# A decoder layer on one core: TensorE sums the last block's squares at the boundaries itself, and two planned waits get shorter

## The chip, the core and the metric

One NeuronCore of a Trainium2 chip runs the whole kernel. The metric is the device time of one execution in microseconds; the median of three executions is 1598.87 us (1598.24 to 1599.2). The core has a matrix engine (TensorE, PE in the profile, with its weight loads as PEld), three engines for elementwise work (VectorE or DVE, ScalarE or ACT, GpSimd or POOL), and SyncE (SP), which here issues DMAs. Each engine takes its instructions in order; between engines they wait for one another by semaphores.

## The reference

One layer of a decoder for 512 prompt tokens and 8 x 4 sample tokens, model width 1024, all in float32, with an RMS norm before and after each of three sub-layers and a shift, scale and gate from a conditioning vector:

```
x += 1/2 * gate1 * post1( SwiGLU1( mod1(pre1(x)) ) )
h  = mod2(pre2(x)); p = h @ w_in
   branch A: gated DeltaNet (conv, decay, delta rule)    branch B: sliding-window attention
   y = sigmoid(gate_A) * o_A + sigmoid(gate_B) * o_B
x += gate2 * post2( y @ w_out )
x += 1/2 * gate3 * post3( SwiGLU2( mod3(pre3(x)) ) )

def rmsnorm(x, gain):
    y = x * lax.rsqrt(jnp.mean(x * x, axis=-1, keepdims=True) + EPS)
    return y * gain
```

What bears on the change is the mean of squares over the 1024 features of a token, at each post and each pre norm after the first.

## The kernel before

Activations lie transposed, features on partitions: 8 blocks of 128 features by 544 tokens (`xT`). The tokens are worked in two halves of 272 (TH), c = 0 and c = 1; the second half holds the 32 sample tokens. A matrix product in float32 is made of three matmuls: weights arrive by DMA (`raw`), ScalarE rounds them to `hi`, VectorE or GpSimd forms `lo` = raw - hi (line 271), and `mm3` (line 301) adds hi x xh, hi x xl and lo x xh in PSUM. In the profile `pd` is the down projection of a feed-forward network, `pg` and `pu` are its gate and up projections, `pb` the projections of the mixer, `adaps` the projection of the conditioning vector.

A sub-layer's output is gathered in `dacc` block by block. After each block `sumsq` (line 516) squares it on ScalarE (`sqt`), and adds the square to `sqd`, a tile of 128 partitions by 544 tokens: blocks 0 to 6 on GpSimd, block 7 on VectorE (line 525). When block 7 is done, `boundary` (line 578) is started for that half of the tokens. It runs in this order:

- `rms` (line 357) on `sqd`: three matmuls with 128 tokens of `sqd` as weights against a column block of ones sum over the partitions (`post_s`, line 366); VectorE forms mean plus EPS (`rmsx`) and eleven small steps of a reciprocal square root (`rms3y`, `rms3a`, lines 334 to 345); TensorE turns the roots round and spreads them over the partitions (`post_p`, lines 353 and 355).
- `residual` (line 555): for each block VectorE forms `mt` and adds it to `xT`, ScalarE squares the new `xT`, and the square is added to `sqx`, blocks 0 to 6 on GpSimd, block 7 on VectorE.
- `rms` on `sqx` (`pre_s`, `pre_p`), then `modulate` (line 527), which makes the split input `hh`, `hl` of the next projection.

This happens twice for each half: after the first feed-forward network (about 440 to 520 us) and after the mixer (about 1130 to 1190 us). In the program the norms are called post2, pre3, post5 and pre6. The end of the layer (`Last.finish`, line 761, about 1542 us for c = 0 and 1579 us for c = 1) has the sums and roots of post8 and then the outputs `yo`. `xnps` and `dnps` are transposes for the output.

The order of the instructions is written by a planner, `Streams` (line 145). The main stream of projection units runs, and side streams, such as a boundary, are taken up when they are due: each `yield cost, latency` adds cost to a model clock and makes the stream due again after 1.5 times the latency. So the latency of a yield says how many units of the main stream are put between two steps of a side stream. In `rms` the yield between sums and transposes is `yield 0.7, 3.0`; in `residual` each block has `yield 0.0, 0.8`; between residual and the second norm stands `yield 0.0, 1.0`. GpSimd also clears tiles for the mixer's inverse (`X`, `XL`, lines 1389 and 1390), of which `X` waits for the last `mt` of the first boundary.

Of the kernel before, what the change touches and what calls it, by code (L numbers as in the profile page):

```python
# [19 lines left out]
P = 128  # L20
# [26 lines left out]
NDOWN = 7  # L47
NFRONT = 5
# [188 lines left out]
class Layer:  # L237
# [118 lines left out]

    def rms(self, sq, cs, name):


        nc = self.nc  # L360
        ps = self.wk(name + "_s")
        n = 3 * len(cs)
        s3 = ps[:, :n * 64].rearrange("p (c n) -> p c n", n=64)
        for i, c in enumerate(cs):
            for j, o in enumerate((0, P, TH - P)):
                nc.tensor.matmul(out=s3[:, 3 * i + j, :], lhsT=sq[:, c * TH + o:c * TH + o + P], rhs=self.ones[:, :64],
                                 start=True, stop=True)
        x = self.st.tile([P, 6], F32, tag="rmsx", name="rmsx")[:, :n]
        nc.vector.tensor_scalar(out=x, in0=s3[:, :, 0], scalar1=1.0 / D, scalar2=EPS, op0=ALU.mult, op1=ALU.add)
        r = self.rsqrt(x, [P, n], "rms%d" % n)  # L370
        yield 0.7, 3.0
        out = []
        e = 2 * P - (TH - P)
        for i in range(len(cs)):
            rp = self.wk(name + "_p")
            self.bcast_cols(r, [(3 * i, 0, P), (3 * i + 1, 0, P), (3 * i + 2, e, P)],
                            [rp[:, :P], rp[:, P:2 * P], rp[:, 2 * P:TH]], name)
            out.append(rp[:, :TH])
        yield 0.6, 0.4
        return out  # L380
# [134 lines left out]

    def sumsq(self, x, sq, b, tmp, c, eng=None):

        nc = self.nc
        s = slice(c * TH, (c + 1) * TH)
        if b == 0:  # L520
            nc.scalar.activation(out=sq[:, s], in_=x[:, s], func=AF.Square)
        else:
            t = tmp.tile([P, TH], F32, tag="v", name="sqt", bufs=V_BUFS)
            nc.scalar.activation(out=t, in_=x[:, s], func=AF.Square)
            (eng or nc.gpsimd).tensor_tensor(out=sq[:, s], in0=sq[:, s], in1=t, op=ALU.add)

# [28 lines left out]
    def residual(self, rp, d, gseg, tmp, sqx, c):  # L555

        nc = self.nc
        o, n = c * TH, TH - c * NS
# [8 lines left out]
        for b in range(8):  # L567
            t = tmp.tile([P, TH], F32, tag="u", name="mt", bufs=U_BUFS)
            nc.vector.scalar_tensor_tensor(out=t[:, :n], in0=d[:, b, s], scalar=self.modT[:, gseg, b, 0:1],
                                           in1=rp[:, :n], op0=ALU.mult, op1=ALU.mult)  # L570
            nc.vector.tensor_tensor(out=self.xT[:, b, s], in0=self.xT[:, b, s], in1=t[:, :n], op=ALU.add)  # L571
            self.sumsq(self.xT[:, b, :], sqx, b, tmp, c, nc.vector if b == 7 else None)
            yield 0.0, 0.8

    def boundary(self, sqd, d, gseg, seg, tmp, sqx, x, c, done, after=None):

        rp, = yield from self.rms(sqd, (c,), f"post{gseg}")
        yield from self.residual(rp, d, gseg, tmp, sqx, c)
        if after:
            after(c)  # L580
        yield 0.0, 1.0
        rp, = yield from self.rms(sqx, (c,), f"pre{seg}")
        yield from self.modulate(rp, seg, tmp, x, c)
        done.add(c)


    def ffn(self, pre, x, env, front, ndown, hook, each=None):
# [3 lines left out]
        nc, a = self.nc, self.a  # L591
# [63 lines left out]
        def down(half, b, cs):  # L655
# [3 lines left out]
            for k0 in (0, 4, 8):  # L659
                def go(w, k0=k0):  # L660
# [16 lines left out]
                    for c in cs:  # L677
                        self.sumsq(d[:, b, :], sqd, b, tmp, c, nc.vector if b == 7 else None)
                        if each:
                            each(b, c)  # L680
                        if b == 7:
                            hook(c)
                nk = 4 if k0 < 8 else 3
# [30 lines left out]
class Last:  # L714
# [45 lines left out]

    def finish(self, c, pss):
        nc, L, a = self.nc, self.L, self.L.a
        ps = L.wk("post8_s")
        s3 = ps[:, :192].rearrange("p (c n) -> p c n", n=64)
        for i, o in enumerate(self.OFF):
            nc.tensor.matmul(out=s3[:, i, :], lhsT=self.sqd[:, c * TH + o:c * TH + o + P], rhs=L.ones[:, :64],
                             start=True, stop=True)
        v = L.st.tile([P, 3], F32, tag="rmsx", name="rmsx")
# [1023 lines left out]
def layer(ctx, tc, a, dbg=None, stop=None):  # L1792
# [19 lines left out]

    def hook1(c):
        sch.spawn(L.boundary(sqd, env["d"], 2, 3, tmp, sqx, x, c, done), c)

# [47 lines left out]
    def main():  # L1863
# [23 lines left out]
        def useh(b, c):  # L1887
            def f(ps):
                dd, sq, t = bufs["d"], bufs["sqd"], bufs["tmp"]
                nc.scalar.copy(out=dd[:, b, c * TH:(c + 1) * TH], in_=ps[:, c, :TH])  # L1890
                L.sumsq(dd[:, b, :], sq, b, t, c, nc.vector if b == 7 else None)
                if b == 7:
                    sch.spawn(L.boundary(sq, dd, 5, 6, t, bufs["sqx"], x, c, done,
                                         lambda c: sch.spawn(last[0].turn_x(c), 2)), c)
            return f
# [43 lines left out]
        last.append(Last(L, tmp, d, bufs["sqd"], hp, fp))  # L1939
        feed.add(L.ffn("ffn2", x, bufs, NFRONT, NDOWN, lambda c: sch.spawn(last[0].finish(c, last[0].ps), 0), last[0].block))  # L1940
        yield from feed.run(mo)
# [34 lines left out]
```

## Time and profile before

| | before |
|---|---|
| median of three executions | 1598.87 us (1598.24 to 1599.2) |
| the profiled execution, its own time | 1593.05 us |
| its span, first to last instruction | 1591.2 us |
| mean granted clock of TensorE | 0.985 |
| TensorE busy | 1517.3 us (95%) |
| VectorE busy | 853.9 us (54%) |
| ScalarE busy | 633.7 us (40%) |
| GpSimd busy | 288.3 us (18%) |

The profile is of one execution. An engine's busy share is an average over stages with different limits. In a row of a timeline the first number is the start within the span, the second the length, `x3` the number of instructions drawn together, and the bracket the idle time before them with what ended it. The granted clock 1.00 is TensorE's full speed, 2.4 GHz; a mean below it over a stretch is a share of the stretch at 1.2 GHz.

### The profile page before, as it was taken

How to read it: one execution, taken by the hardware profiler on the slowest of the kernel's cores; microseconds unless marked ns; L12 is line 12 of the kernel's file. 1: busy time of each engine (PE TensorE's matmuls, PEld its weight loads, DVE VectorE, ACT ScalarE, POOL GpSimd, SP SyncE). 2: the span in 40 equal slices, each digit the busy share in tenths (PEclk: the TensorE clock that was granted, in tenths of full speed). 3: DMA queues.
4: the chain of work that ended last, by engine and by line, in shares of the span. 5: the costliest groups of instructions: out<-in, count | busy, mean ns of one | idle time of the engine just before them, and what ended most of it. 6: DMA issues, size and time to landing. Idle time of an engine off the chain costs nothing. (4 is left out here: it accounts for less than half of the span.)

```text
span 1591.2 us, 32547 instructions
## 1 busy us (share of the span) xinstructions
PE 1517.3 (95%) x12851; PEld 1406.0 (88%) x12851; DVE 853.9 (54%) x2080; ACT 633.7 (40%) x1397; POOL 288.3 (18%) x395
## 2 busy tenths in 40 slices
PE   7999999999998999999999998998979999999996
PEld 3799999999987999997788997897979999999995
DVE  5433322333588778578789556756474332233365
ACT  4322222322445553455485242233455332223363
POOL 2000000000343232131021023131548000000042
PEclk9999999999999999999999999999999999999998
DMA  9564445455556434753112324614425432333253
GB/s 317 162 193 134 152 142 157 141 159 157 173 158 189 119 82 100 174 143 85 45 44 68 93 81 126 179 49 133 139 67 161 108 87 86 91 90 90 80 154 112
DMA packets 314528, 199.66 MB, mean 125 GB/s; under 512 B 36596, under 2 KB 297295, under 8 KB 314086
## 3 DMA queue, kind: packets, MB, share of 16 engines
q1 hardware_dynamic: 314086, 197.46, 43.8%
q8 instruction: 101, 1.65, 0.4%
q14 instruction: 53, 0.43, 0.1%
q0 software_dynamic: 288, 0.11, 0.0%
HBM read 182.08 MB, written 16.36 MB: 125 GB/s over the span
## 5 line engine op out<-in xcount | busy, mean ns | idle before, releaser
L270 ACT CAST hi<-raw 128x512 fp32r<-128x512 f32 (+2 forms) x502 | 287.9, 581 | 608.9 <-PE pu L301 171.6
L271 DVE TENSOR_TENSOR lo<-raw,hi 128x512 fp32r<-128x512 f32 (+2 forms) x368 | 253.7, 690 | 391.8 <-ACT hi L270 383.1
L301 PE MATMUL pb<-hh,hi 128*128 128x272 f32 (+1 forms) x1008 | 233.6, 302 | 4.1 <-ACT hh L270 3.0
L301 PE MATMUL pb<-hl,hi 128*128 128x272 f32 (+1 forms) x1008 | 225.5, 293 | 3.2 <-DVE hl L271 3.2
L271 POOL TENSOR_TENSOR lo<-raw,hi 128x512 fp32r<-128x512 f32 (+1 forms) x104 | 137.0, 1321 | 498.0 <-ACT hi L270 465.2
L301 PE MATMUL pb<-hh,lo 128*128 128x272 f32 (+1 forms) x1008 | 224.1, 293 | 0.2
L301 PEld LDWEIGHTS pb<-hh,hi 128*128 128x128 f32 (+1 forms) x1008 | 163.7, 190 | 16.9 <-issue 7.2
L301 PE MATMUL pd<-fh,hi 128*128 128x272 f32 x704 | 172.0, 291 | 0.0
L301 PE MATMUL pd<-fl,hi 128*128 128x272 f32 x704 | 170.7, 289 | 0.0
L301 PEld LDWEIGHTS pb<-hl,hi 128*128 128x128 f32 (+1 forms) x1008 | 164.2, 190 | 5.4 <-DVE hl L271 3.6
L301 PE MATMUL pd<-fh,lo 128*128 128x272 f32 x672 | 163.1, 290 | 3.3 <-DVE lo L271 2.7
L301 PEld LDWEIGHTS pb<-hh,lo 128*128 128x128 f32 (+1 forms) x1008 | 162.9, 190 | 2.3 <-DVE lo L271 0.8
L301 PE MATMUL pg<-hh,hi 128*128 128x272 f32 x672 | 150.0, 293 | 7.3 <-ACT hh L538 3.6
L301 PE MATMUL pu<-hh,hi 128*128 128x272 f32 x672 | 148.4, 291 | 0.0
L301 PE MATMUL pg<-hl,hi 128*128 128x272 f32 x672 | 147.1, 290 | 0.3 <-DVE hl L539 0.2
L301 PE MATMUL pu<-hl,hi 128*128 128x272 f32 x672 | 146.4, 289 | 0.0
L301 PE MATMUL pu<-hh,lo 128*128 128x272 f32 x672 | 145.5, 288 | 0.7 <-POOL lo L271 0.7
L301 PE MATMUL pg<-hh,lo 128*128 128x272 f32 x672 | 145.6, 288 | 0.0
L301 PEld LDWEIGHTS pd<-fh,hi 128*128 128x128 f32 x704 | 120.5, 189 | 8.6 <-issue 4.2
L301 PEld LDWEIGHTS pg<-hh,hi 128*128 128x128 f32 x672 | 109.0, 189 | 20.3 <-issue 5.0
L301 PEld LDWEIGHTS pd<-fl,hi 128*128 128x128 f32 x704 | 120.9, 189 | 0.0
L301 PEld LDWEIGHTS pd<-fh,lo 128*128 128x128 f32 x672 | 114.6, 189 | 5.1 <-DVE lo L271 3.7
(455 smaller groups left out, 2510.6 us busy)
## 6 DMA issues: line engine op xcount, KB each, us to landing
raw<-w_in SPq DMA_DIRECT2D x136, 256.0 KB, 3.1
wa<-w_ada SPq DMA_DIRECT2D x56, 512.0 KB, 4.3
raw<-ffn_w_gate SPq DMA_DIRECT2D x94, 256.0 KB, 2.9
raw<-ffn_w_up SPq DMA_DIRECT2D x94, 256.0 KB, 2.9
raw<-ffn_w_down SPq DMA_DIRECT2D x92, 256.0 KB, 3.0
wb<-w_ada SPq DMA_DIRECT2D x32, 256.0 KB, 6.3
S<-state_delta SPq DMA_DIRECT2D x8, 512.0 KB
delta_sample<-S SPq DMA_DIRECT2D x8, 512.0 KB, 5.4
```

The costliest lines, as they stand in the source:

```text
L270: self.nc.scalar.copy(out=hi, in_=raw)
L271: (eng or self.nc.vector).tensor_tensor(out=lo, in0=raw, in1=hi.bitcast(F32), op=ALU.subtract)
L301: self.nc.tensor.matmul(out=ps[:m, c, :TH], lhsT=a[:r, kt, :m], rhs=b[:r, kx, c * TH:(c + 1) * TH], start=first and i == 0, stop=last and ...
```

## The change

At block 7 the square is no longer added to `sqd` or `sqx`. It stays in its own tile, and `rms` gets it as `extra`: after each of the three sum matmuls a second one with `extra` as weights adds into the same columns of PSUM. This holds at ten places: post2, pre3, post5, pre6 and post8, each for both halves. So ten additions on VectorE are gone (six into `sqd`, four into `sqx`) and thirty matmuls are new. The first norm of the kernel is as before. Three latencies of the planner are smaller: 3.0 to 2.0 between sums and transposes, 0.8 to 0.7 for each block of the residual, 1.0 to 0.6 between residual and second norm. They apply to the boundaries; with them, and since the plan's clock runs otherwise, the steps of the boundaries stand at other places among the projections.

```diff
@@ def rms
-    def rms(self, sq, cs, name):
+    def rms(self, sq, cs, name, extra=None):
...
                 nc.tensor.matmul(out=s3[:, 3 * i + j, :], lhsT=sq[:, c * TH + o:c * TH + o + P], rhs=self.ones[:, :64],
-                                 start=True, stop=True)
+                                 start=True, stop=extra is None)
+                if extra is not None:
+                    nc.tensor.matmul(out=s3[:, 3 * i + j, :], lhsT=extra[:, o:o + P], rhs=self.ones[:, :64],
+                                     start=False, stop=True)
...
-        yield 0.7, 3.0
+        yield 0.7, 2.0
@@ def sumsq
-    def sumsq(self, x, sq, b, tmp, c, eng=None):
+    def sumsq(self, x, sq, b, tmp, c, eng=None, alone=False):
...
             nc.scalar.activation(out=t, in_=x[:, s], func=AF.Square)
+            if alone:
+                return t
             (eng or nc.gpsimd).tensor_tensor(out=sq[:, s], in0=sq[:, s], in1=t, op=ALU.add)
@@ def residual, def boundary
-            self.sumsq(self.xT[:, b, :], sqx, b, tmp, c, nc.vector if b == 7 else None)
-            yield 0.0, 0.8
-
-    def boundary(self, sqd, d, gseg, seg, tmp, sqx, x, c, done, after=None):
-
-        rp, = yield from self.rms(sqd, (c,), f"post{gseg}")
-        yield from self.residual(rp, d, gseg, tmp, sqx, c)
+            t = self.sumsq(self.xT[:, b, :], sqx, b, tmp, c, alone=b == 7)
+            yield 0.0, 0.7
+        return t
+
+    def boundary(self, sqd, extra, d, gseg, seg, tmp, sqx, x, c, done, after=None):
+
+        rp, = yield from self.rms(sqd, (c,), f"post{gseg}", extra)
+        t = yield from self.residual(rp, d, gseg, tmp, sqx, c)
         if after:
             after(c)
-        yield 0.0, 1.0
-        rp, = yield from self.rms(sqx, (c,), f"pre{seg}")
+        yield 0.0, 0.6
+        rp, = yield from self.rms(sqx, (c,), f"pre{seg}", t)
         yield from self.modulate(rp, seg, tmp, x, c)
         done.add(c)
@@ def ffn, after a block of the down projection
-                        self.sumsq(d[:, b, :], sqd, b, tmp, c, nc.vector if b == 7 else None)
+                        t = self.sumsq(d[:, b, :], sqd, b, tmp, c, alone=b == 7)
...
-                            hook(c)
+                            hook(c, t)
@@ Last.finish
-    def finish(self, c, pss):
+    def finish(self, c, pss, extra):
...
-                             start=True, stop=True)
+                             start=True, stop=False)
+            nc.tensor.matmul(out=s3[:, i, :], lhsT=extra[:, o:o + P], rhs=L.ones[:, :64], start=False, stop=True)
@@ the output of the mixer, and the three places that start a boundary or the end, hand the tile on
-                L.sumsq(dd[:, b, :], sq, b, t, c, nc.vector if b == 7 else None)
+                e = L.sumsq(dd[:, b, :], sq, b, t, c, alone=b == 7)
...
```

Two places in the new order. VectorE at the end of the modulation of half 0 at the first boundary, about 482 to 490 us in the profile before; `mt` and `hl` belong to the modulation, `dacc` is the accumulation of a block of half 1, `sqd` the addition of its last square, and `rmsx` the first step after the sum of post2 of half 1. Before:

```order
L536 SCALAR_TENSOR_TENSOR mt<-xT,modT,pre_p 128x272 x3
L539 SCALAR_TENSOR_TENSOR hl<-mt,modT,hh 128x272 x3
L271 TENSOR_TENSOR lo<-raw,hi 128x512
L536 SCALAR_TENSOR_TENSOR mt<-xT,modT,pre_p 128x272
L676 TENSOR_TENSOR dacc<-pd,dacc 128x272
L539 SCALAR_TENSOR_TENSOR hl<-mt,modT,hh 128x272
L525 TENSOR_TENSOR sqd<-sqd,sqt 128x272
L369 TENSOR_SCALAR rmsx<-post_s 128x3
```

After:

```order
L544 SCALAR_TENSOR_TENSOR hl<-mt,modT,hh 128x272 x2
L541 SCALAR_TENSOR_TENSOR mt<-xT,modT,pre_p 128x272 x3
L271 TENSOR_TENSOR lo<-raw,hi 128x512
L544 SCALAR_TENSOR_TENSOR hl<-mt,modT,hh 128x272 x3
L682 TENSOR_TENSOR dacc<-pd,dacc 128x272 x2
L372 TENSOR_SCALAR rmsx<-post_s 128x3
```

Both last accumulations into `dacc` now stand behind the modulation, directly ahead of the root, and the addition is gone.

GpSimd at the end of the residual of half 1 at the first boundary, about 500 to 510 us before; `sqx` are the additions of the squares of blocks 1 to 5 and of block 6, `X` and `XL` the tiles that are cleared for the mixer, `lo` a subtraction for a block of weights. Before:

```order
L271 TENSOR_TENSOR lo<-raw,hi 128x512 x3
L525 TENSOR_TENSOR sqx<-sqx,sqt 128x272 x5
L1389 MEMSET X 128x1024
L525 TENSOR_TENSOR sqx<-sqx,sqt 128x272
L1390 MEMSET XL 128x512
L271 TENSOR_TENSOR lo<-raw,hi 128x512
```

After:

```order
L271 TENSOR_TENSOR lo<-raw,hi 128x512
L530 TENSOR_TENSOR sqx<-sqx,sqt 128x272 x5
L1396 MEMSET X 128x1024
L1397 MEMSET XL 128x512
L271 TENSOR_TENSOR lo<-raw,hi 128x512
L530 TENSOR_TENSOR sqx<-sqx,sqt 128x272
```

The addition of block 6 now stands behind both clearings and a subtraction; before, only the first clearing stood ahead of it.

## Rows read from the trace of the kernel before

**Rows 1.** The page, busy time, share of the span and instructions of each engine:

```profile
PE 1517.3 (95%) x12851; PEld 1406.0 (88%) x12851; DVE 853.9 (54%) x2080; ACT 633.7 (40%) x1397; POOL 288.3 (18%) x395
```

**Rows 2.** The view of line 525: who waited for its additions (us, times):

```profile
  PE post_s L366: 3.4, 3
...
  PE post_s L766: 2.1, 2
  PE pre_s L366: 2.1, 1
```

**Rows 3.** Stretches: length, busy time (instructions), PEclk, share of DMA, GB/s:

```profile
460.00:470.00 10.00, 8.48 (x49) 7.51 (x49) 8.63 (x15) 5.79 (x15) 7.01 (x7) 0.83 0.57 164
...
1170.00:1180.00 10.00, 6.19 (x31) 5.25 (x30) 9.41 (x16) 6.14 (x13) 7.39 (x9) 0.68 0.38 105
```

**Rows 4.** Timeline of PE, 443 to 471 us: start, length, [idle before]; then by line, 440 to 480:

```profile
443.07 0.88 PE L366 MATMUL post_s<-ones,sqd 128*128 128x64 f32 x6 [0.24 <-DVE sqd L525]
...
448.61 0.38 PE L353 MATMUL post_p<-ident,rms3y 128*128 128x128 f32 x2
...
470.54 0.78 PE L366 MATMUL pre_s<-ones,sqx 128*128 128x64 f32 x6
471.13 0.37 PE L301 MATMUL pd<-fh,hi 128*128 128x272 f32 x1
...
L301 PE MATMUL pd<-fh,lo 128*128 128x272 f32 x72 | 21.8, 303 | 2.2 <-DVE lo L271 2.1
```

**Rows 5.** Timeline of DVE, 446 us:

```profile
446.25 1.22 DVE L343 SCALAR_TENSOR_TENSOR rms3a<-rmsx,rms3y 128x3 f32<-128x3 f32 x1
```

**Rows 6.** Timeline of POOL, 446 us:

```profile
446.16 1.29 POOL L271 TENSOR_TENSOR lo<-raw,hi 128x512 fp32r<-128x512 f32 x1 [5.44 <-ACT hi L270]
```

**Rows 7.** Timeline of PE, 485 to 494 us:

```profile
485.66 1.05 PE L467 MATMUL adaps<-wa,cT 128*32 128x512 f32 x4 [1.10 <-DMA wa<-w_ada]
...
493.83 0.43 PE L353 MATMUL post_p<-ident,rms3y 128*128 128x128 f32 x2 [1.16 <-DVE rms3y L345]
```

**Rows 8.** Timeline of DVE, 477 to 487 us:

```profile
477.70 1.31 DVE L536 SCALAR_TENSOR_TENSOR mt<-xT,modT,pre_p 128x272 f32<-128x272 f32 x3 [0.24 <-PE pre_p L355]
...
486.41 0.50 DVE L539 SCALAR_TENSOR_TENSOR hl<-mt,modT,hh 128x272 fp32r<-128x272 f32 x1 [0.24 <-ACT hh L538]
```

**Rows 9.** Timeline of PE, 509 to 514 us:

```profile
509.20 0.88 PE L366 MATMUL pre_s<-ones,sqx 128*128 128x64 f32 x6 [2.06 <-DVE sqx L525]
...
513.70 0.43 PE L353 MATMUL pre_p<-ident,rms3y 128*128 128x128 f32 x2 [0.30 <-DVE rms3y L345]
```

**Rows 10.** Timeline of POOL, 507 to 510 us:

```profile
507.00 0.95 POOL L1389 MEMSET X<- 128x1024 f32 x1 [0.70 <-DVE mt L569]
507.91 0.76 POOL L525 TENSOR_TENSOR sqx<-sqx,sqt 128x272 f32<-128x272 f32 x1
508.61 0.53 POOL L1390 MEMSET XL<- 128x512 f32 x1
509.09 1.27 POOL L271 TENSOR_TENSOR lo<-raw,hi 128x512 fp32r<-128x512 f32 x1
```

**Rows 11.** Timeline of PE at the second boundary, 1136 to 1189 us:

```profile
1136.53 0.88 PE L366 MATMUL post_s<-ones,sqd 128*128 128x64 f32 x6 [1.69 <-DVE sqd L525]
...
1156.02 0.88 PE L366 MATMUL post_s<-ones,sqd 128*128 128x64 f32 x6 [1.47 <-DVE sqd L525]
...
1176.39 0.59 PE L301 MATMUL pg<-hh,hi 128*128 128x272 f32 x1 [1.69 <-ACT sil L607]
...
1183.55 0.77 PE L366 MATMUL pre_s<-ones,sqx 128*128 128x64 f32 x6
...
1189.24 0.43 PE L353 MATMUL pre_p<-ident,rms3y 128*128 128x128 f32 x2 [0.25 <-DVE rms3y L345]
```

**Rows 12.** Timeline of POOL, 1135 us:

```profile
1135.22 0.77 POOL L525 TENSOR_TENSOR sqd<-sqd,sqt 128x272 f32<-128x272 f32 x1
```

**Rows 13.** Timeline of DVE, 1579 us:

```profile
1578.95 0.44 DVE L525 TENSOR_TENSOR sqd<-sqd,sqt 128x272 f32<-128x272 f32 x1 [0.57 <-ACT sqt L524]
```

More of the change, by code (lines that the diff above doesn't have):

```diff
@@ L1811, in layer, with hook1 @@
     done = set()
-    def hook1(c):
-        sch.spawn(L.boundary(sqd, env["d"], 2, 3, tmp, sqx, x, c, done), c)
+    def hook1(c, t):
+        sch.spawn(L.boundary(sqd, t, env["d"], 2, 3, tmp, sqx, x, c, done), c)
     env = {"tmp": tmp, "sqd": sqd}
@@ L1890, in f @@
                 nc.scalar.copy(out=dd[:, b, c * TH:(c + 1) * TH], in_=ps[:, c, :TH])
-                L.sumsq(dd[:, b, :], sq, b, t, c, nc.vector if b == 7 else None)
+                e = L.sumsq(dd[:, b, :], sq, b, t, c, alone=b == 7)
                 if b == 7:
-                    sch.spawn(L.boundary(sq, dd, 5, 6, t, bufs["sqx"], x, c, done,
+                    sch.spawn(L.boundary(sq, e, dd, 5, 6, t, bufs["sqx"], x, c, done,
                                          lambda c: sch.spawn(last[0].turn_x(c), 2)), c)
@@ L1939, in main @@
         last.append(Last(L, tmp, d, bufs["sqd"], hp, fp))
-        feed.add(L.ffn("ffn2", x, bufs, NFRONT, NDOWN, lambda c: sch.spawn(last[0].finish(c, last[0].ps), 0), last[0].block))
+        feed.add(L.ffn("ffn2", x, bufs, NFRONT, NDOWN, lambda c, t: sch.spawn(last[0].finish(c, last[0].ps, t), 0), last[0].block))
         yield from feed.run(mo)
```

## The prediction

> **What bounds the kernel now.** I read the page's busy line first: TensorE is busy for 1517.3 of 1591.2 us, VectorE for 853.9, GpSimd for 288.3 [rows 1]. On the whole TensorE is the bound, so work that is moved from VectorE to TensorE costs its full price unless it fills time in which TensorE stood idle. Second, I asked the view by line what follows the additions that the change takes off VectorE: TensorE waited for them 3.4 us at the layer's own sums of squares after a projection, 2.1 us at those of the last stage and 2.1 us at those ahead of a projection, 7.6 us at six of the ten places [rows 2]. That is what there is to win directly. Third, the table by stretches tells which engine is full around the places: from 460 to 470 us VectorE is busy 8.63 of 10 us and the granted clock is 0.83; from 1170 to 1180 VectorE is busy 9.41, TensorE 6.19, clock 0.68 [rows 3]. So at the boundaries, and only there, VectorE sets the pace, and a wait that goes at a sum can come back a few microseconds on. The rest of the reading is the timeline at each place.
>
> **The price of the added work.** At each of ten places three more matmuls of 128x128 against 64 columns are issued. Three of the same shape, each with weights of its own, stand at 470.54, and the next matmul at 471.13 [rows 4]: 0.59 us. No row shows one that accumulates; with the same shape and weight loads I take 0.6 us a place, 6.0 us in all (5.9 by this row, 6.9 by the 0.69 us that the places after a wait show, where the first records are stretched). The row counts two records for each matmul. The Trainium skill, FP8 and Floating Point Precision, section TensorE Precision Notes, counts four passes for a true fp32 matmul; 30 matmuls of four passes of 64 columns at 2.4 GHz would be 3.2 us by that (an estimate). It would make the sum below 2.8 us lower, but the interval between starts is measured, and the weights have to be loaded too, so the row decides.
>
> **First boundary, token half 0.** The sum at 443.07 waited 0.24 us for the addition [rows 4]. It goes, but the Square on ScalarE is still needed, so it is all that is won there. The transposes that bring the roots back (448.61 [rows 4]) now stand twelve matmuls sooner in the order, 1.5 us at 0.127 us each (38 of them lie between 443.76, where the three sums were issued, and 448.61). The roots' chain on VectorE cannot follow: its ninth step, from 446.25, lasts 1.22 us, as long as a subtraction that GpSimd runs from 446.16 to 447.45 [rows 5, 6], and with two steps more the chain is done at 447.9 whether it begins a little sooner or not. TensorE would be there at about 447.5, so it waits up to 0.4 us; I take half. Term: +0.6 - 0.24 + 0.2 = +0.6. The residual on VectorE begins about 1 us sooner, but in the new order a split of 0.85 us and one more pair of its operations stand ahead of the next weights; the waits for weights that total 2.1 us between 440 and 480 [rows 4] stay as they are by that count: 0, with -2.1 (all gone) and +1.0 as bounds. The drop of the clock there costs 1.7 us (0.17 of 10 us at half speed [rows 3]); it may go with them. The sum at 470.54 waited for nothing: +0.6.
>
> **First boundary, half 1.** The order moves its first sum from behind two groups of adaLN matmuls to a place ahead of them. Before, TensorE waited 1.10 us for the DMA of those weights and 1.16 us for the roots [rows 7]. In the new order VectorE does both last accumulations into dacc behind the whole modulation of half 0, and the Square of block 6 and its addition on GpSimd follow them. The modulation began at 477.70 and with its last operation ended at 486.9 [rows 8]; now its sum stands ten matmuls sooner, and six matmuls and a pair of the adaLN ones (1 us) no longer stand between sum and transposes: 3.0 us less the 0.6 that the sum itself takes, so it begins 2.4 us sooner, with 0.3 us more of splits in it. It ends at 484.8, dacc is done at 485.2, and with a Square of 0.43 us (an estimate by VectorE's operations of that size) and an addition of 0.77 the sum is ready at about 486.5. TensorE stood at the DMA's wait from 484.5 [rows 7]; the new place is nine matmuls ahead, 1.1 us, and the terms so far delay it by 1.2: 484.6. So a new wait of 1.9 us (0.9 to 3.0), in which the DMA's is hidden, takes the place of the 2.26 us: +0.6 - 2.26 + 1.9 = +0.2. The second sum waited 2.06 us at 509.20 [rows 9]. Its chain was: VectorE's last mt, GpSimd's memset of X (0.95 us, which waits for this mt since it takes over its input's memory), the addition of block 6 (0.76), then the one removed (0.44) [rows 10]. In the new order two more operations of GpSimd stand ahead of block 6's addition: the memset of XL (0.53) and a weight subtraction (1.27) [rows 10]. From the start of the memset to the sum that makes 0.95 + 0.53 + 1.27 + 0.76 = 3.5 us, where it was 2.2 (507.00 to 509.20 [rows 9, 10]): the removed 0.44 us is paid three times over. Against this the residual begins some 3.9 us sooner (transposes at 490 instead of 493.83), so its last mt falls between 499 and 501.3, the sum is ready between 502.6 and 504.9, and TensorE, which was there at 507.14, with the sum some 45 matmuls further up (5.7 us) and 1.4 us of delay, at 502.8: a wait of 0 to 2.1, I take 1.0. The transposes then wait 0.7 instead of 0.30 us [rows 9], as fewer matmuls stand between. Term: +0.6 - 2.06 + 1.0 + 0.4 = 0, between -1.0 and +1.1.
>
> **Second boundary.** The sum at 1136.53 waited 1.69 us [rows 11], but block 6's addition on GpSimd, behind three weight subtractions in its queue, ended only at 1135.99 [rows 12]. So it starts 0.5 us sooner, not 1.2, and loses that to its own 0.6 us. At 1156.02 the wait of 1.47 us [rows 11] is filled by the other half's sums, which the new order puts ahead. All this lies before a stretch that VectorE bounds: TensorE goes on at 1176.39, after 1.69 us for ScalarE's sil [rows 11], which in the new order has one more Square of the residual ahead of it. What is won or lost before falls into that wait: I count +0.3 for the whole stretch up to there (-1.0, if VectorE's two additions of 0.44 us go straight through, to +0.8). At 1183.55 nothing waited [rows 11], and nothing covers the new matmuls: +0.6. The transposes at 1189.24 waited 0.25 us [rows 11] and stand ten rows of work, 1.2 us, sooner, while the chain starts 0.6 us later and meets GpSimd's subtractions as it did at 446 [rows 5, 6]: a wait of about 0.9 instead of 0.25, of which some comes back at a later wait: +0.4. Together +1.0.
>
> **The tail.** At half 0, 1542 us, the smaller of the two waits of 2.1 us [rows 2] pays for the 0.6 us, and a split that moves inside the roots' chain keeps the outputs where they were: 0 (-1 to +1.5). At half 1 nothing follows but the roots and the output. VectorE's addition from 1578.95 to 1579.39 goes [rows 13], and TensorE's sums begin right after the Square, at 1578.9. The three transposes that stood between the sums go behind them, which about pays for the three matmuls: -0.45, the length of the addition.
>
> **The sum.** 0.6 + 0 + 0.6 + 0.2 + 0 + 0.3 + 1.0 + 0 - 0.45 = +2.25 us. On the profiled execution (1593.05 us) that is 1595.3. The median of the runs shown is 5.8 us higher than this execution; the change's terms are the same there: 1598.87 + 2.25 = 1601.1, which is 0.14% more. A difference under 0.2% (3.2 us) cannot be told from none here.
>
> **Rivals.** (a) The waits go and nothing takes their place: 6.0 - 7.6 for the sums, -0.45 at the end as the chain there is VectorE's, and of the 3.8 us of waits and low clock around 460 us about half, since VectorE is rid of two additions and the roots come sooner: -4, at 1595. For it speaks that six of ten places show the wait; against it, that at 1136 and at 509 GpSimd ends last once VectorE's addition is gone. Chance 0.25. (b) Slower: GpSimd's addition of block 6 behind the memsets and the subtraction. Where the last mt falls at 501.3, TensorE waits 2.1 us, not 1.0, and together with the new wait of 2 to 3 us before it the stretch from 484 to 505 has few full microseconds. Around 463 us three waits of this size were followed by a mean clock of 0.83 over ten microseconds [rows 3]; the same again is 1.7 us. The Trainium skill, TensorE: Matmul & The Clock Gate, section A second HAM failure mode, says that short idle times between groups of matmuls make the clock go to and fro between its two levels; the two windows of rows 3 agree. With 1.1 + 1.7 on the sum, and 0.4 more at the transposes of 1189: +5.5, at 1604.3. It decides from a wait above 2 us at the second sum of half 1. Chance 0.33. (c) The forecast, that gains and added work cancel within 3.2 us: 0.42; by itself 1597 to 1602. (That the change doesn't do what it says, in that the order shifts nothing but adds the work, is 6.0 - 7.6 and a few tenths: within (c).)
>
> The range reaches from most of (a) to most of (b): 1594.5 to 1605.5. Faster by over 0.2% 0.25, within 0.2% 0.42, slower by over 0.2% 0.33.
>
> **What would show it.** In the profile after: TensorE's busy time up by about 6 us; VectorE's down by some 4 (ten times 0.44); no wait of TensorE for VectorE's sqd or sqx at the sums, but waits for GpSimd's additions at 509 and 1136 and for a Square or GpSimd at the first sum of half 1; the roots' transposes waiting longer than before; the last roots 0.45 us sooner after the last accumulation. I am wrong if the second sum of half 1 waits for nothing, if the clock does not fall around 463 any more, or if the resumption at 1176 comes more than a microsecond sooner or later against the stretch before it.

## The result, and the profile after

| | before | after |
|---|---|---|
| median of four executions | 1599.03 us (1598.24 to 1602.68) | 1613.75 us (1612.61 to 1615.17) |
| the profiled execution, its own time | 1593.05 us | 1612.61 us |
| mean granted clock | 0.985 | 0.978 |

The ratio is 1.009 (95% interval 1.0072 to 1.0108): 14.7 us slower, above the range of the prediction. (Executions of the kernel before, in this and the later comparisons, spread from 1593 to 1606 us, and the first profile of it is of a short one. So whole kernels are compared by several executions of each, and single profiles stretch by stretch.)

The page's busy line of after, which answers to [rows 1]:

```profile
PE 1532.1 (95%) x12911; PEld 1421.6 (88%) x12911; DVE 849.0 (53%) x2070; ACT 634.3 (39%) x1397; POOL 290.3 (18%) x395
```

VectorE lost its ten additions (853.9 to 849.0 us), TensorE has 60 more records (two for each of 30 matmuls). Its busy time grew by 14.8 us, not by the 6 of the new matmuls: where the granted clock is at 1.2 GHz, a matmul is busy for longer (0.43 instead of 0.29 us in the rows below).

To see where the time went I took the start of the same matmul in both traces and subtracted. After lies 0.3 us behind before at 480 us and 0.1 at 500, then 7.1 at 530, 6.8 at 560; 12.1 at 1110 and 13.8 at 1130; 17.9 at 1240; 18.2 at 1535 and 19.8 at the end. After was already 0.6 us behind at 435, so the first boundary (435 to 560) costs 6.2 us, and all of it falls between 500 and 530; the second (1130 to 1240) costs 4.1 and the tail 1.6. The rest arises in the mixer, where both kernels have the same instructions in the same order (taken up below, with a second profile of each).

TensorE at the second sum of half 1 of the first boundary, which answers to [rows 9] (start, length, then in the bracket the idle time before the row and what ended it):

```profile
505.97 0.69 PE L366 MATMUL pre_s<-ones,sqx 128*128 128x64 f32 x2 [4.40 <-POOL sqx L530]
506.45 0.63 PE L369 MATMUL pre_s<-ones,sqt 128*128 128x64 f32 x2
...
508.16 0.64 PE L369 MATMUL pre_s<-ones,sqt 128*128 128x64 f32 x2
508.55 0.57 PE L301 MATMUL pb<-hh,lo 128*128 128x272 f32 x1
508.93 0.43 PE L301 MATMUL pb<-hh,hi 128*128 128x272 f32 x1
```

TensorE came to the sum at 501.57 and stood for 4.40 us, where it had waited 2.06 before. What follows runs at half the clock: six matmuls from 505.97 to 508.55 (2.58 us; six take 1.25 to 1.3 at full clock, as below), and projections 0.23 us apart instead of 0.13 up to 512.10. The stretches show it (length, busy time and instructions of PE, PEld, DVE, ACT, POOL, then the granted clock, DMA share, GB/s):

```profile
500.00:510.00 10.00, 5.45 (x28) 5.01 (x27) 5.23 (x13) 2.76 (x7) 5.82 (x8) 0.77 0.78 285
510.00:520.00 10.00, 9.29 (x65) 8.75 (x63) 7.83 (x26) 5.56 (x13) 0.90 (x2) 0.89 0.34 88
```

The same two stretches before:

```profile
500.00:510.00 10.00, 7.84 (x61) 7.40 (x60) 8.30 (x14) 5.91 (x14) 8.99 (x10) 1.00 0.55 139
510.00:520.00 10.00, 9.70 (x78) 8.79 (x78) 8.74 (x32) 5.03 (x13) 1.77 (x6) 1.00 0.84 290
```

GpSimd at the same place, which answers to [rows 10]:

```profile
500.88 1.30 POOL L530 TENSOR_TENSOR sqx<-sqx,sqt 128x272 f32<-128x272 f32 x1 [0.93 <-ACT sqt L527]
502.12 0.95 POOL L1396 MEMSET X<- 128x1024 f32 x1
503.01 0.52 POOL L1397 MEMSET XL<- 128x512 f32 x1
503.50 1.26 POOL L271 TENSOR_TENSOR lo<-raw,hi 128x512 fp32r<-128x512 f32 x1
504.72 1.20 POOL L530 TENSOR_TENSOR sqx<-sqx,sqt 128x272 f32<-128x272 f32 x1
```

The first row is the addition of block 5, which itself stood 0.93 us for a Square. From there on there is no gap: from 502.12 to 505.92 GpSimd is busy with what the new order put ahead of block 6's addition, and with the addition, which takes 1.20 us, not 0.76, while VectorE runs a subtraction of 1.48 us beside it. All waits of TensorE above 0.3 us between 440 and 540 us sum to 6.8 us before and 7.8 after: the waits did not go, they were gathered into one.

The second boundary, which answers to [rows 11]. TensorE of after:

```profile
1148.43 0.43 PE L366 MATMUL post_s<-ones,sqd 128*128 128x64 f32 x2 [0.39 <-POOL sqd L530]
...
1191.93 0.59 PE L301 MATMUL pg<-hh,hi 128*128 128x272 f32 x1 [2.58 <-ACT sil L613]
...
1205.04 0.43 PE L353 MATMUL pre_p<-ident,rms3y 128*128 128x128 f32 x2 [1.42 <-DVE rms3y L345]
...
1218.60 0.39 PE L301 MATMUL pg<-hh,hi 128*128 128x272 f32 x1 [1.40 <-ACT sil L613]
```

The waits at the sums are gone or small (0.39 instead of 1.69 and 1.47), and three later ones have grown: for `sil` 2.58 (1.69 before) and 1.40 (0.49), for the roots of half 1 1.42 (0.25). All above 0.3 us from the first sum on: 9.8 us before, 11.2 after. The clock is down for longer: 0.83, 0.91 and 0.75 in the three tens from 1170 to 1200, where before had 0.68, 0.98 and 1.00. The new matmuls are 0.66 us a place (four places, 2.6 us).

The tail: at half 0 a new wait of TensorE, for a split of weights on VectorE that now stands behind two outputs `yo` in a row; it was 0.31 us before. VectorE's split, then TensorE:

```profile
1569.11 1.75 DVE L271 TENSOR_TENSOR lo<-raw,hi 128x512 fp32r<-128x512 f32 x1
...
1570.91 0.40 PE L301 MATMUL pd<-fh,lo 128*128 128x272 f32 x1 [2.28 <-DVE lo L271]
```

At half 1, VectorE from the last accumulation to the first step of the root, where [rows 13] had its addition; first before, then after:

```profile
1577.94 0.44 DVE L676 TENSOR_TENSOR dacc<-pd,dacc 128x272 f32<-128x272 f32 x1 [2.91 <-PE pd L301]
...
1580.65 0.16 DVE L769 TENSOR_SCALAR rmsx<-post_s 128x3 f32<-128x3 f32 x1 [1.16 <-PE post_s L766]
```

```profile
1597.71 0.44 DVE L682 TENSOR_TENSOR dacc<-pd,dacc 128x272 f32<-128x272 f32 x1 [2.91 <-PE pd L301]
...
1600.03 0.16 DVE L776 TENSOR_SCALAR rmsx<-post_s 128x3 f32<-128x3 f32 x1 [1.19 <-PE post_s L774]
```

2.71 us before, 2.32 after. So 0.39 us are won there.

### The profile page after: what moved, and what is told of

It reads as the page before. It is cut to its first block, busy times and chain, and to the rows that moved or that the text cites. A ratio compares the mean times of both kernels' runs of the same rounds, so it can differ in the third digit from the quotient of the medians.

```text
span 1610.8 us, 32652 instructions
## 1 busy us (share of the span) xinstructions
PE 1532.1 (95%) x12911; PEld 1421.6 (88%) x12911; DVE 849.0 (53%) x2070; ACT 634.3 (39%) x1397; POOL 290.3 (18%) x395
## 4 chain that ended last, share of the span: by engine, by line
PE 78%; DVE 11%; DMA 4%; ACT 2%; issue 2%; POOL 2%; SPq 0%; DVEq 0%; ACTq 0%; POOLq 0%
PE pb L301 18%; PE pg L301 16%; PE pu L301 15%; PE pd L301 14%; PE adaps L470 3%; DVE y L1202 1%; DVE lo L271 1%; PE psc L1017 1%; DMA raw<-ffn_w_down 1%; PE pgu L301 1%; PE pov L1073 1%; POOL lo L271 1%; PE pkq L1289 1%; ACT hi L270 1%; DVE X L1430 1%
```

## The experiments

Below, "behind" is always the start of the same matmul minus that in the first profile of before, what a boundary costs is read between the same times as above, and medians are compared with those of before on the same chip (1599.7 in the first two sets, 1600.0 in the third).

**The new sums with the old latencies.** In the kernel after:

```diff
-        yield 0.7, 2.0
+        yield 0.7, 3.0
-            yield 0.0, 0.7
+            yield 0.0, 0.8
-        yield 0.0, 0.6
+        yield 0.0, 1.0
```

> The changed kernel with the three latencies of the planner as before (3.0, 0.8, 1.0): all thirty new matmuls, but block 6's addition of half 1 at the first boundary stands on GpSimd ahead of the clearing of X and XL instead of behind it and a weight subtraction. Theory A (the place of that addition, brought about by the shorter latencies, makes most of the loss): TensorE waits under 1.5 us at the second sum of half 1 (4.40 in the changed kernel), the granted clock from 500 to 520 us is 1.0 (0.77 and 0.89 there), and the time is 0 to 5 us over before. Theory B (the new matmuls make the loss, at 0.22 us each 6.6 us and what they push back): 8 to 15 us over before, about as the changed kernel.

1606.15 us, ratio 1.0042 (1.0026 to 1.0058). At the second sum of half 1:

```profile
508.12 0.69 PE L366 MATMUL pre_s<-ones,sqx 128*128 128x64 f32 x2 [3.19 <-POOL sqx L530]
```

The wait did not fall below 1.5 us as I had expected, and the clock was 0.90 and 0.76 in the two tens from 500 to 520. Here block 6's addition is ahead of the clearings again, but GpSimd's last two additions had to wait for a Square (0.93 us, from 505.4) and ended at 508.06, while TensorE stood there from 504.93: the residual itself is later than the sum. The first boundary costs 5.5 us, the second only 0.2, the tail 1.7.

**The latencies alone.** The same three numbers, the other way, in the kernel before; no new matmuls.

> The kernel before with the three shorter latencies alone; all squares are added as before, no new matmul. On GpSimd only the clearing of X stands between the additions of blocks 5 and 6, as before. Theory A (place of block 6's addition): the second sum of half 1 at the first boundary waits 2 to 3.5 us, as the residual begins sooner and X is cleared only after its last mt; time within 5 us of before either way. Theory B (the matmuls make the loss): at or below before, by up to 4 us. A third, C (sooner transposes and the later stretch at the second boundary make the loss): 4 us or more over before, with the waits for the roots at the second boundary longer.

1607.89 us, ratio 1.0053 (1.0034 to 1.0071). In total time the two halves of the change add up, 0.42% and 0.53% against 0.90% for both; place by place, as the figures below show, they do not. TensorE at the second boundary has the three grown waits of after, without a single new sum:

```profile
1182.75 0.60 PE L301 MATMUL pg<-hh,hi 128*128 128x272 f32 x1 [2.58 <-ACT sil L607]
...
1195.80 0.43 PE L353 MATMUL pre_p<-ident,rms3y 128*128 128x128 f32 x2 [1.41 <-DVE rms3y L345]
...
1209.37 0.40 PE L301 MATMUL pg<-hh,hi 128*128 128x272 f32 x1 [1.40 <-ACT sil L607]
```

This is the third of the outcomes that I had put down. So these waits come from the order, not from the added work; in the run with the new sums and the old latencies they are 2.19, 0.27 and 0.49 us. At the first boundary the wait at the second sum of half 1 is 2.59 us, followed by a clock of 0.83 from 510 to 520, and 3.6 us are lost there; the second boundary loses 2.1 and the tail 0.4. Against 6.2, 4.1 and 1.6 for the whole change, the new sums alone lose 5.5, 0.2 and 1.7: the tail's loss is theirs, either half by itself loses at the first boundary, and at the second it takes the shorter latencies.

**Only the latency between sums and transposes as before.** In the kernel after, 2.0 back to 3.0, the other two as they are.

> The changed kernel with the latency between sums and transposes as before (3.0 for 2.0); the two others stay short (0.7 and 0.6). Theory F (at the second boundary this one latency makes the loss, since it puts the transposes of half 1 ahead of a chain of roots that GpSimd stretches, and the first modulation ahead of the second roots): the wait at pre6's transposes of half 1 falls from 1.42 to under 0.5 us, the wait for sil from 2.58 to about 2 us, and the stretch from 1130 to 1240 us loses under 1.5 us against the kernel before (4.5 in the changed kernel). Rival: the two other latencies do it; then the stretch still loses 3.5 us or more. At the first boundary block 6's addition stands behind the clearing of X alone: a wait of 2.5 to 4 us and a low clock, loss 4 to 6 us there.

1605.28 us, ratio 1.0053 (1.0028 to 1.0078). The wait for the roots of half 1 at the second boundary is gone, and those for `sil` are 2.20 and 0.65 (2.58 and 1.40 in after); the wait at the second sum of half 1 at the first boundary is 2.85. The second boundary loses 1.5 us, the first 3.6. Of the 14.7 us this one number gives back some 9 by the medians, 6 by the ratios and 5 by the two boundaries; the intervals of the two kernels just overlap, so the size is not settled.

**Block 6's addition on VectorE.** In the kernel after, only for half 1 of the first boundary:

```diff
-            t = self.sumsq(self.xT[:, b, :], sqx, b, tmp, c, alone=b == 7)
+            t = self.sumsq(self.xT[:, b, :], sqx, b, tmp, c, nc.vector if (b, c, gseg) == (6, 1, 2) else None, alone=b == 7)
```

> The changed kernel with one addition moved: block 6's square of half 1 at the first boundary is added on VectorE instead of behind the clearings and the subtraction on GpSimd. Everything else is as in the changed kernel. Theory A: the wait of 4.40 us at the second sum of half 1 falls below 1.5 us, the clock from 500 to 520 us is back at 1.0, and the time falls by 5 to 8 us against the changed kernel, to 1605 to 1609. Theory B: the wait goes, but the time stays within 2 us of the changed kernel, as the same time is lost on the roots or the weights next.

1613.94 us, ratio 1.0091 (1.0076 to 1.0106): no gain. VectorE's last additions to `xT`, TensorE, and the stretches:

```profile
502.95 1.28 DVE L576 TENSOR_TENSOR xT<-xT,mt 128x240 f32<-128x240 f32 x2
...
505.03 0.57 PE L366 MATMUL pre_s<-ones,sqx 128*128 128x64 f32 x2 [2.78 <-DVE sqx L530]
```

```profile
500.00:510.00 10.00, 7.12 (x38) 6.68 (x38) 6.45 (x18) 3.65 (x9) 5.64 (x8) 0.76 0.77 274
510.00:520.00 10.00, 9.26 (x63) 8.52 (x62) 7.96 (x25) 5.90 (x13) 1.23 (x2) 0.90 0.47 125
```

GpSimd's queue is out of it, and still 2.78 us are left: the residual's last `xT` ends at 504.2, and TensorE is there at 502.25. The clock is as low as with 4.40. Between 500 and 530 us 5.3 us are lost instead of 7.0, and the second boundary loses 7.1. GpSimd's queue was the last to arrive, but behind it the sum simply stands too early for the residual.

**The sum held back.** In the kernel after, the second norm of half 1 at the first boundary is put 29 rows of TensorE later:

```diff
+                self.mms = getattr(self, 'mms', 0) + 1        # in mm3, for each matmul
...
         yield 0.0, 0.6
+        while (gseg, c) == (2, 1) and self.mms < 3225:
+            yield 0.0, 0.2
```

> The changed kernel; only the second norm of half 1 at the first boundary is held back in the plan until the projections of half 0 have come 32 matmuls (4 us) further, so that TensorE has work while GpSimd clears its tiles and adds block 6. Nothing is computed otherwise. Theory D (the 7 us lost at 500 to 530 us are a wait that comes of hoisting the sum, 2.5 us, and the half clock that follows it, 2.9 us; in the test before, the wait fell from 4.40 to 2.78 us, the clock still fell, and nothing was won): with a wait under 1 us the granted clock from 500 to 520 us is 1.0, the lag behind the kernel before at 530 us falls from 7 to under 3 us, and the time is 1607 to 1610. Theory E (the loss comes of the six matmuls of the sum and of VectorE's backlog): the clock may stay up, but the lag at 530 us is still 5 us or more and the time 1612 or more.

1610.01 us, ratio 1.0073 (1.0047 to 1.0099). TensorE:

```profile
505.73 0.39 PE L302 MATMUL pb<-hh,lo 128*128 128x272 f32 x1 [1.55 <-POOL lo L271]
507.85 0.33 PE L367 MATMUL pre_s<-ones,sqx 128*128 128x64 f32 x2
...
515.22 0.40 PE L302 MATMUL pb<-hh,hi 128*128 128x272 f32 x1 [1.74 <-ACT hi L270]
516.58 0.39 PE L302 MATMUL pb<-hh,lo 128*128 128x272 f32 x1 [0.84 <-POOL lo L271]
```

Nothing waits at the sum any more, the clock is 1.00 from 500 to 510, and between 480 and 530 us 3.1 us are lost instead of 6.8 (at 530 this profile is 4.6 behind, where I had expected under 3). So about 3.7 us of the loss hung on where this one sum stands. Three waits for splits of weights, 4.1 us in all, stand there now: the first is new, the two others were 0.71 and 0.45 us in the kernel after. The clock is 0.87 from 510 to 520. In total time the gain is 3.7 us by the medians too, but the intervals of the two kernels overlap.

**The tail alone, and its half 1 alone.** In the kernel before, new sums at post8 of both halves; then at half 1 only. `rms` and `sumsq` as in the change, the other places hand on nothing:

```diff
-                        self.sumsq(d[:, b, :], sqd, b, tmp, c, nc.vector if b == 7 else None)
+                        t = self.sumsq(d[:, b, :], sqd, b, tmp, c, nc.vector if b == 7 and pre == 'ffn1' else None, alone=b == 7 and pre != 'ffn1')
```

(for half 1 only, with `and c == 1` at the last condition, and the addition on VectorE kept for c = 0)

> The kernel before with the new sums only in the last stage (post8, both halves); boundaries and latencies as before. Prediction: at half 0 nothing won, at half 1 -0.45 us from the last accumulation to the roots; time within 1.5 us of before. Theory A' (in the changed kernel the last stage lost 1.9 us, of which 2.3 us is one wait for a weight subtraction that stands behind two outputs at half 0): the same wait appears here, and the time is 1 to 2.5 us over before. Rival: the wait comes from where the weights' loads stood after the earlier delays; then it is not here, and the time is 0.5 us under before.

> The kernel before with the new sum at one place alone: post8 of half 1, the last of the kernel, where nothing but the roots and the outputs follows. Prediction: 0.3 to 0.6 us from the last accumulation into dacc to the first step of the roots are won, and the order up to there is as before, so that the time is 0.2 to 0.6 us under before, which the timing alone can't tell from none. Rival: the six matmuls take as long as VectorE's addition and nothing is won; the interval from dacc to rmsx stays at 2.7 us.

Both halves: 1600.4 us, ratio 1.0003 (0.9986 to 1.0019); half 1 only: 1599.16, ratio 0.9996 (0.9982 to 1.001). Neither can be told from before by its time, so the profiles must say it. With both, the wait of after appears, and the tail costs 1.6 us, as in after:

```profile
1558.18 0.40 PE L301 MATMUL pd<-fh,lo 128*128 128x272 f32 x1 [2.26 <-DVE lo L271]
```

With half 1 alone TensorE waits 0.55 us there (0.31 before), the tail costs nothing, and from the last accumulation to the root it takes 2.33 us (1584.34 to 1586.67), 0.38 less than before.

**Sixteen columns.** In the kernel after, all sums against 16 columns of ones instead of 64 (`[:, :16]` for `rhs` and `out`).

> The changed kernel with 16 columns of ones instead of 64 in the sums, both the old and the new matmuls of them. It tells what a sum's matmul is bound by. Theory G (by loading its weights, 128x128 in float32, which takes as long whatever the columns): the interval between two of these matmuls stays at 0.2 to 0.23 us, six of them still take 1.3 to 1.5 us, and the time stays within 2 us of the changed kernel. Rival H (by the columns that stream): the interval falls below 0.12 us, a place costs 0.7 us less, and the time falls by 5 us or more.

1613.6 us, ratio 1.0091 (1.0063 to 1.012). The sums of the tail:

```profile
1600.04 0.39 PE L774 MATMUL post_s<-ones,sqt 128*128 128x16 f32 x2 [0.87 <-ACT sqt L527]
1600.28 0.37 PE L772 MATMUL post_s<-ones,sqd 128*128 128x16 f32 x2
1600.51 0.37 PE L774 MATMUL post_s<-ones,sqt 128*128 128x16 f32 x2
```

They stand 0.22 to 0.24 us apart, as with 64 columns (1598.94, 1599.16, 1599.38 in after). What a sum costs here is not its columns. A weight load of it lasts 192 ns in both kernels; that this load sets the interval was not varied by itself and is not shown.

**A second profile of each kernel.** Both unchanged.

> The kernel before, unchanged, for a second profile. Between 560 and 1110 us, where the two kernels run the same instructions in the same order, the first profile of after lost another 6 us on the first profile of before. Theory M: that is one execution against another; then this profile too lies 2 to 9 us behind the first one at 1110 us, with less granted clock in 540 to 1120, while it lies within 1 us at 530 us and has the same waits there. Theory N: the later boundary causes it; then this profile stays within 1 us of the first one up to 1110 us.

> The kernel after, unchanged, for a second profile. Both theories: the wait at the second sum of half 1 is 4.4 within 0.3 us, and the first boundary costs 6.7 within 1 us against the first profile of before. Theory M (the loss in the mixer is one execution's own): the loss between 560 and 1110 us comes out more than 2 us away from the first one's 6. Theory N (it follows from the order): 6 within 1 us again.

Before: 1598.47 us; after: 1611.23. How far each profile lies behind the first one of before:

| at us | 435 | 530 | 560 | 1110 | 1130 | 1240 | 1535 | end |
|---|---|---|---|---|---|---|---|---|
| before, second | 1.6 | 2.8 | 2.7 | 7.3 | 6.2 | 5.3 | 5.3 | 5.4 |
| after, first | 0.6 | 7.1 | 6.8 | 12.1 | 13.8 | 17.9 | 18.2 | 19.8 |
| after, second | 0.4 | 6.6 | 6.3 | 12.5 | 11.4 | 16.4 | 16.4 | 18.4 |

From 560 to 1110 us before loses 4.6 us on its own first profile, after 5.3 and 6.2; the other kernels, all with the same order there, lost 0.5 (the latencies alone) to 9.0 (the roots' latency as before). So the mixer's 5 to 6 us are mostly the first profile of before, which passed there quickly. I had expected the second profile of after to differ from its first by more than 2 us if that was so; it did not. But the five profiles of kernels with the boundary of before lose 0 to 6.7 us, 4.2 on average, and those of after, of block 6 on VectorE, of the sum held back and of the sixteen columns 2.2 to 6.2, 4.6 on average: no loss of the change in the mixer can be told from this spread. The wait at the sum repeats (4.39 after, 2.07 before):

```profile
505.91 0.69 PE L366 MATMUL pre_s<-ones,sqx 128*128 128x64 f32 x2 [4.39 <-POOL sqx L530]
```

That row is of after, the next of before, each in its second profile:

```profile
510.95 0.88 PE L366 MATMUL pre_s<-ones,sqx 128*128 128x64 f32 x6 [2.07 <-DVE sqx L525]
```

In this profile of before a wait of 2.07 us was followed by a clock of 0.83 from 510 to 520, in the first one, after 2.06, by 1.00. Three other profiles with before's order at this place waited 2.08 to 2.09 us and kept 1.00. Against the second profile the first boundary costs 4.8 to 5.1 us and the second 5.0 to 5.9.

**What might beat before: block 6 at the second boundary, and a later sum.** The kernel with the new sum at half 1 of the tail only, and block 6's addition at post5 of half 0 on VectorE; then the same with the second sum of half 1 at the first boundary 14 rows later.

```diff
-                e = L.sumsq(dd[:, b, :], sq, b, t, c, nc.vector if b == 7 else None)
+                e = L.sumsq(dd[:, b, :], sq, b, t, c, nc.vector if b == 7 or (b, c) == (6, 0) else None)
```

```diff
         yield 0.0, 1.0
+        while (gseg, c) == (2, 1) and self.mms < 3260: yield 0.0, 0.2
```

> The kernel before, with the new sum only in the tail's half 1 (worth 0.4 us) and block 6's addition of the second boundary's half 0 on VectorE, which waits 7.9 us there behind GpSimd's queue. Theory Q (the queue of GpSimd is what these places wait for): both additions end by 1135.4 instead of 1136.5, TensorE's wait there falls from 1.69 to 0.4 to 0.7 us, and the kernel takes 1597.6, 1.0 to 1.6 us below before (ratio 0.9990 to 0.9994, hardly to be resolved). Theory R (what is gained comes back at the next wait): the wait shrinks, and the time stays within 0.3 us of before.

> The kernel of the run before this one, and in it the second sum of half 1 at the first boundary stands 14 rows later in TensorE's order (a change of the planner's release, which also reorders some 90 rows of VectorE after it). Theory Q: the wait of 2.06 there falls under 0.5, and as in the run with the sum held back no clock is lost by it: 1596, another 1.5 us less (ratio 0.998). Theory R: waits for splits that come later take its place (there 1.55 and 1.74 of them), and the time stays that of the run before this one within 0.5 us.

The first: 1597.57 us against 1600.03, ratio 0.9987 (0.9974 to 1.0000). The fastest median of all, but its interval ends at no change. TensorE's sum and VectorE's two additions:

```profile
1142.21 0.88 PE L366 MATMUL post_s<-ones,sqd 128*128 128x64 f32 x6 [0.93 <-DVE sqd L530]
```

```profile
1139.56 1.16 DVE L530 TENSOR_TENSOR sqd<-sqd,sqt 128x272 f32<-128x272 f32 x1 [4.95 <-POOL lo L271]
1140.89 1.27 DVE L530 TENSOR_TENSOR sqd<-sqd,sqt 128x272 f32<-128x272 f32 x1 [0.17 <-ACT sqt L527]
```

The wait fell from 1.69 to 0.93, not to 0.4 to 0.7: the additions last 1.16 and 1.27 us, not 0.44, while GpSimd runs its three subtractions (1137.87 to 1141.86), and the first of them still waited for GpSimd.

The second: 1598.99 us, ratio 1.0000 (0.9985 to 1.0015). The sum waits for nothing, and two waits for splits (1.51 and 1.57 us, at 518.40 and 520.27) take its place; between 500 and 530 us this profile loses 3.2 us, which the kernel without this delay does not lose. As in the kernel after, a sum put later hands its wait on to the weights; here that costs more than it saves.

## Why the prediction was wrong

**The step that failed** is the second sum of half 1 at the first boundary, "a wait of 0 to 2.1, I take 1.0 ... Term: +0.6 - 2.06 + 1.0 + 0.4 = 0". Measured, TensorE fell 7.0 us further behind between 500 and 530. By its parts: three more matmuls 0.7; the wait 4.40 instead of 2.06, 2.3; the half clock 2.8 (the six matmuls of the sum take 2.58 instead of 1.3 us, and the 3.55 us up to 512.10 do what takes 2.0 at full clock); two waits for splits behind it, 0.71 and 0.45, 1.2; less the 0.30 at the transposes: 6.7, which is what is left at 560.

The chain named, GpSimd's memsets and subtraction ahead of block 6's addition, was the last to arrive; it was counted at 3.5 us and took 3.8. What was wrong is where both sides start. The last `mt` ended at 500.96, as foretold, but I let the memsets begin with it, between 499 and 501.3, and they began at 502.12: GpSimd was busy with block 5's addition up to then, which had waited for a Square of its own. And TensorE was there at 501.57 instead of 502.8, as the wait of 1.9 us that I put ahead of it was 0.73 (0.51 and 0.22). Both errors make the wait longer. And a second thing stood behind the chain: without GpSimd's queue the wait was still 2.78 us, since the sum had been moved ahead of the residual's own end.

The rival that saw this decide "from a wait above 2 us" was right in kind, at 2.8 us for the place more than forecast, and too small. Three runs bear on the cause, all at this one place: without GpSimd's queue 2.78 us of wait remain and 5.3 of the 7.0 us lost, with the sum 29 rows later neither wait nor some 3.7 us of the loss, and the old latencies bring 3.19. So the mechanism I named is a part, 1.7 us at this place and nothing in the total; where the sum stands against the residual is the larger one. Of the 3.1 us that are still lost with the sum held back, 0.7 are the new matmuls; the rest goes with the waits for weights and the clock of 0.87 behind them, which no run separates.

**The clock** was priced at 1.7 us from the earlier place [rows 3], where three waits of 0.67, 0.49 and 0.98 us, none of them of 2 us, came before the drop. After 4.40 us it cost 2.8, with 0.77 and 0.89 granted from 500 to 520. The Trainium skill, TensorE: Matmul & The Clock Gate, section A second HAM failure mode, tells of a bf16 kernel whose clock goes to and fro where TensorE idles briefly between groups of matmuls; this trace agrees in that the clock fell with the one wait (0.77 and 0.89) and was back at 1.00 behind it. My sign that I would be wrong "if the clock does not fall around 463 any more" came true too, on the good side: there the waits are 0.36, 0.32 and 0.66 us instead of 2.1 in all, the clock is 1.00, and from 435 to 480 after gains 0.3 us instead of losing 1.2. (In the run with block 6 on VectorE, which has the same order there and nearly the same waits, the clock from 460 to 470 was 0.83 again.)

**The price of a sum** was right in kind. Where the six matmuls wait for nothing they take 1.25 us:

```profile
467.29 0.33 PE L366 MATMUL pre_s<-ones,sqx 128*128 128x64 f32 x2
...
468.54 0.37 PE L301 MATMUL pd<-fh,hi 128*128 128x272 f32 x1
```

Three took 0.59, so it is 0.66 us a place, 6.6 us in all instead of 6.0, and the columns play no part in it, as the run with 16 shows. The lower estimate that the prediction weighed and left, 3.2 us, would have been half of it.

**The new wait at the first sum of half 1** was smaller than 1.9; its term was right within half a microsecond (0.2 gained where +0.2 stood).

**The second boundary** was put at +1.3 and cost 4.1 and 5.0 in the two profiles of after. It is the second step that failed. That block 6 on GpSimd ends last at 1136 held (`POOL sqd`, 0.39 us). "What is won or lost before falls into that wait" failed: the wait for `sil` did not take the loss up but grew by 0.9, TensorE goes on at 1191.93, 1.7 us later against the stretch before (my sign that I would be wrong, from a microsecond on), and a second wait for `sil` grew by 0.9. The latencies alone make both. The transposes' wait was put at 0.9 and was 1.42.

**The tail.** Half 1 was right: 0.45 foretold, 0.39 and 0.38 measured. Half 0 was put at 0, "a split that moves inside the roots' chain keeps the outputs where they were". They did not stay: the first output begins 6.66 us after the last accumulation instead of 5.60, the next split comes behind two outputs in a row and lasts 1.75 us, and TensorE waits 2.28 us for it. The tail as a whole costs 1.6 (2.0 in the second profile) instead of -0.45.

The sum by these measurements, on the first profiles: -0.3 up to 480, -0.2 to 500, 6.7 to 560, 4.1, 1.6: 12 us; the medians say 14.7. Single profiles of one order differ by as much as the rest: at the second boundary the five profiles with the order of after lose 4.1, 5.0, 7.6, 7.1 and 4.2 us, so that the first of them is the lowest, and those with before's order lie between -1.0 and 0.9. With their mean of 5.6 us there, 6.4 at the first boundary (6.2, 5.9 and, with 16 columns, 7.1) and 1.6 to 2.0 in the tail it is about 14 us, which leaves little to place.

## What to carry to other kernels

An operation that is taken off a chain's end gains nothing where another queue ends right behind it: look at each input of the waiting instruction, and at what the new order puts ahead of each in its own queue. A planner's latency is a promise on when inputs are ready; made smaller than the chain takes (here 3.0 to 2.0), it moves the waiting instruction up and turns covered time into a wait. Moving such an instruction back down is not sure to help: in the kernel after it gave back about 3.7 us around the sum, in the kernel before the same move cost 3.2, as waits for weights took its place.

## What was not expected of the hardware

- Waits of the same length did not always bring the clock down: 2.07 us was followed by 0.83 over ten microseconds, 2.06 us by 1.00, in two executions of one kernel. The longer ones at this sum (2.59 to 4.40, in seven profiles) all came with a clock of 0.66 to 0.83 over the ten microseconds from the sum's start.
- An fp32 sum of 128x128 against 64 or 16 columns takes 0.22 to 0.24 us either way.
- Additions of 128x272 on VectorE took 1.16 and 1.27 us beside GpSimd's subtractions and 0.44 alone. By the Trainium skill, SBUF — State Buffer, section Who interferes with whom, a VectorE instruction with two inputs in SBUF contends with a GpSimd instruction that reads there; the trace agrees with these numbers.
- One kernel passes through the same 550 us of the mixer in times that differ by 4.6 us from one execution to the next; fourteen profiles of kernels with the same order there differ by up to 9.0.
